# A two-layer hybrid trunk on one core: gate and GLU projections streamed 512 columns wide, first-layer tables built beside the transposes, output stages re-timed

## The chip, the cores and the metric

The kernel runs on one core of a Trainium2 chip. The metric is the device time of one execution in microseconds (us), lower is better. Four engines matter here: PE (TensorE, matrix products and 128x128 transposes), DVE (VectorE), ACT (ScalarE) and SP (SyncE, which issues the transfers). Every engine works through its own instructions strictly in the order in which the program lists them; an instruction that waits holds up all that stand behind it on its engine.

## What is computed

Two layers of the same form run on x, 256 positions by 2048 channels, in float32:

```python
for l in range(2):
    h = rmsnorm(x, pre_norm_g[l])
    proj = h @ w_in[l]                                  # 2048 x 6144
    q, k, v, z_att, u, z_ssm = split(proj)              # 1024 columns each
    o_att = rmsnorm(diff_attention(q, k, v)) * silu(z_att)
    y = s5_ssm(u, ...)                                  # a scan over the positions
    g_val, g_gate = split(gelu(y) @ w_glu[l])           # 1024 x 2048
    o_ssm = g_val * sigmoid(g_gate) * silu(z_ssm)
    x = x + rmsnorm(concat(o_att, o_ssm) @ w_out[l])    # 2048 x 2048
```

The state space branch takes four positions as one chunk. Tables made from its parameters lead from a chunk of u to the state (`wi`, the chunk-input table), through the state by 62 scan steps (`H`), and from the state to the outputs (`gc`, the output tables).

## The kernel before

All weights are streamed once. A layer's weights are cut into 144 **half chunks** of 128x1024 elements (`hs` in the code, `s` within a layer). Products are made at nearly float32 accuracy from two rounded parts: ACT copies a half chunk into `hi` (`emit_hi`), DVE subtracts that from the raw data into `lo` (`emit_lo`), and PE multiplies with three products (hi by hi, hi by lo, lo by hi) (`main`). The main loop, from line 1143, writes out for each half chunk s: the transfer of half chunk s+6, ACT's `hi` and DVE's `lo` of s+2, PE's products of s, and between them pieces of all other work. So `lo` of s+2 has to be finished by the time PE comes to s+2.

The segments of a layer, by half chunk: u 0 to 15, q 16 to 31, k 32 to 47, v and z_att 48 to 79, z_ssm (`zs`) 80 to 95, glu 96 to 111, out 112 to 143. There are two forms of product. In the segments u (mostly), q, k, zs and glu of the kernel before, a half chunk takes 24 products with 256 moving columns; the result has the channels on the partitions. In v, z_att and out, a half chunk takes 12 products with 512 moving columns, with the activations as the stationary side; the result has the positions on the partitions.

The other work is written as generators. Those in `gens` are advanced once per half chunk, either ahead of `lo` (`run_first`) or, where they yield a number, behind the products of the half chunk (`run_second`, with room 4). Operations on DVE that are long in sum stand in the queue `weave`, first in first out, and are let in between the two halves of `lo` by a budget in ns (`BUDS`, line 1111; `fill`, line 212): the parameters, `z_ops`, `g_ops` (12 operations that make the output tables) and `scan_ops` (62 steps of four operations).

The chain of the state space branch in layer 0: `prep_gen` (line 480) loads B and C, transposes C (`psc`), has `z_ops` made, transposes them to the chunk-input table (`psw`, one block of four transposes behind each of eight half chunks) and only then puts `g_ops` into the weave. `s_gen` waits for the table, makes the inputs of the scan (`pss`) and puts `scan_ops` into the weave behind `g_ops`. `y_gen` (line 742, four pieces j, started from half chunk `Y0` on) multiplies states by output tables (`psy`, `psz`), applies the GELU on ACT and DVE into a tile `y` of which there is one buffer, transposes it on PE (`psg`), and splits it to `ghi` and `glo`, the inputs of glu. `pv_gen` makes the attention output (`pwt`, `wt`, `po`). `evac` takes the finished sums of a segment out of PSUM; for zs and glu it does so once per 128 channels.

Of the kernel before, what the change touches and what calls it, by code (L numbers as in the profile page):

```python
# [27 lines left out]
Y0 = (78, 78)  # L28
# [30 lines left out]
def hybrid_trunk(ctx: ExitStack, tc, x, rel_bias, pre_norm_g, post_norm_g, w_in, lambda_q1, lambda_k1,  # L59
# [105 lines left out]
    for l in range(DEPTH):  # L165
# [13 lines left out]
    def emit_dma(hs):  # L179
# [300 lines left out]
    def prep_gen(l, slots, w_first):  # L480
# [13 lines left out]
        for _ in range(4):  # L494
            yield
# [26 lines left out]
        if not w_first:  # L522
            weave.append(g_ops(l, ccv, tcn, gslots))
# [17 lines left out]
        if not w_first:  # L541
            yield from until("g" + K)
        wi = []
        while l and not S["wfree"]:
            yield
        for b in range(8):
            if b % 4 == 0:
                wi.append(R(wslots[b // 4], "wi"))
            yield 1
            ps = side("psw")  # L550
            for pp in range(2):
                m = 4 * b + 2 * pp
                for a in range(2):
                    tpose(ps[:, 128 * (2 * pp + a):128 * (2 * pp + a) + 128],
                          zt[m // 16][:, 1024 * a + 64 * (m % 16):1024 * a + 64 * (m % 16) + 128], ident)
            yield
            psv = ps.rearrange("p (h a g q) -> p h a g q", h=2, a=2, g=2)
            wv = wi[b // 4].rearrange("p (b h r a q) -> p b h r a q", b=4, h=2, r=2, a=2)[:, b % 4]
            for r in range(2):
                for g in range(2):  # L560
                    act(wv[64 * g:64 * g + 64, :, r], psv[64 * r:64 * r + 64, :, :, g], AF.Copy)
            if l and b == WB - 1:
# [3 lines left out]
        if w_first:  # L566
            weave.append(g_ops(l, ccv, tcn, gslots))
# [174 lines left out]
    def y_gen(l, j):  # L742
        H, U = S["H"], S["U"]
        gc = S[f"gc{l}"][j // 2].rearrange("p (k q a c) -> p k q a c", k=4, q=4, a=2)[:, 2 * (j % 2):2 * (j % 2) + 2]
        yield from until(f"yt{l}{j - 1}" if j else f"h{l}")
        yield 2
# [30 lines left out]
        S[f"yt{l}{j}"] = True  # L777
        yield 1
# [112 lines left out]
    def evac(l, seg, b, ac):  # L891
# [13 lines left out]
        elif seg == "za":  # L905
# [5 lines left out]
            for t in range(2):  # L911
                c0 = 1024 * t + 512 * (b // 4)
                stt(S["za"][:, c0:c0 + 512], th[t], 1.0, ac[t], ALU.add, ALU.mult)
# [29 lines left out]
    def main(hs, only=None):  # L943
# [26 lines left out]
        elif seg in ("u", "q", "k", "zs"):  # L970
# [11 lines left out]
        elif seg == "glu":  # L982
            assert f"y{l}3" in S
            if h == 0:
                S["acc"] = [acc("acg")]
            o = S["acc"][0][:, 256 * h:256 * h + 256]
            hv = hi.rearrange("p (k c) -> p k c", k=8)
            lv = lo.rearrange("p (k c) -> p k c", k=8)
# [271 lines left out]
```

## Time and profile before

| | us |
|---|---|
| median of 3 runs | 942.68 (941.54 to 942.83) |
| profiled execution | 943.94 |
| its span in the trace | 942.2 |

The granted TensorE clock was 0.994 over the span. Busy shares by the page: PE 98%, weight loads 89%, DVE 74%, ACT 52%. The recorded length of a product is not what it costs in a stream: the next one starts before it ends, so costs on PE are read here from start to start.

### The profile page before, as it was taken

To read this page: it belongs to the slowest core of one execution; us is meant where nothing else is said; L and a number is where in the kernel's file an instruction comes from. 1 tells how busy PE (TensorE), PEld (TensorE's weight loads), DVE (VectorE), ACT (ScalarE), POOL (GpSimd) and SP (SyncE) were. 2 spreads that over 40 slices of the span, in tenths; PEclk is the share of its full clock that TensorE was granted. 3 is DMA by queue.
4 is the path that set the end of the run, shared out by engine and by line. 5 is a ranking of instruction groups with operands and counts; after the bars stand their busy time and mean duration, and the time that the engine had idled before them with its cause. 6 is when DMAs were issued, how large, how long until landed. Compare 5 with 4: busy or idle time off the path is not lost.

```text
span 942.2 us, 19053 instructions
## 1 busy us (share of the span) xinstructions
PE 921.2 (98%) x7458; PEld 841.5 (89%) x7458; DVE 694.0 (74%) x1653; ACT 489.4 (52%) x887; POOL 17.2 (2%) x26
## 2 busy tenths in 40 slices
PE   9999999999999999999999999999999999999995
PEld 8999999878789999888889999998888989998884
DVE  4898549899996756887877439999966566665564
ACT  6633375454356557444469343335565655744451
POOL 3000000000000000000000000000000000000001
PEclk9999999999999999999999999999999999999998
DMA  9988665545554498667646856665555446575862
GB/s 299 211 247 221 193 197 168 180 148 166 168 161 129 128 199 240 188 197 268 219 160 192 235 161 184 194 185 162 174 160 178 123 128 180 165 233 183 275 194 89
DMA packets 230458, 176.24 MB, mean 187 GB/s; under 512 B 36471, under 2 KB 190641, under 8 KB 229473
## 3 DMA queue, kind: packets, MB, share of 16 engines
q1 hardware_dynamic: 230016, 174.90, 63.0%
q8 instruction: 58, 0.95, 0.4%
q14 instruction: 32, 0.25, 0.1%
q0 software_dynamic: 352, 0.13, 0.1%
HBM read 167.39 MB, written 7.88 MB: 186 GB/s over the span
## 4 chain that ended last, share of the span: by engine, by line
PE 86%; DVE 7%; ACT 2%; SPq 1%; DMA 1%; issue 1%; DVEq 0%; ACTq 0%
PE ac L113 68%; PE acg L113 9%; DVE lo L116 3%; PE pss L113 2%; DVE sc L116 1%; PE acu L113 1%; PE lga L113 1%; PE po L113 1%; DMA raw<-in_w_in_dram 1%; SPq L489 1%; PE psy L113 1%; PE psw L97 1%; DMA cn<-in_ssm_c_re_dram 1%; ACT hi L134 0%; DVE y L123 0%
## 5 line engine op out<-in xcount | busy, mean ns | idle before, releaser
L134 ACT ACTIVATE hi<-raw 128x1024 fp32r<-128x1024 f32 (+1 forms) x282 | 297.3, 1057 | 366.9 <-PE ac L113 292.7
L116 DVE TENSOR_TENSOR lo<-raw,hi 128x512 fp32r<-128x512 f32 (+1 forms) x400 | 360.3, 904 | 112.4 <-ACT hi L134 111.3
L113 PE MATMUL ac<-hthi,hi 128*128 128x256 f32 x992 | 286.3, 289 | 0.0
L113 PE MATMUL ac<-htlo,hi 128*128 128x256 f32 x992 | 281.6, 284 | 0.2
L113 PE MATMUL ac<-hthi,lo 128*128 128x256 f32 x992 | 281.4, 284 | 0.0
L113 PEld LDWEIGHTS ac<-hthi,hi 128*128 128x128 f32 x992 | 191.1, 193 | 1.3 <-ACT hthi L134 0.3
L113 PEld LDWEIGHTS ac<-htlo,hi 128*128 128x128 f32 x992 | 191.2, 193 | 0.7 <-DVE htlo L123 0.7
L113 PEld LDWEIGHTS ac<-hthi,lo 128*128 128x128 f32 x992 | 190.9, 192 | 0.0
L113 PE MATMUL ac<-lo,hthi 128*128 128x512 f32 x256 | 100.6, 393 | 2.4 <-DVE lo L116 2.4
L113 PE MATMUL ac<-hi,hthi 128*128 128x512 f32 x256 | 102.4, 400 | 0.0
L113 PE MATMUL ac<-hi,htlo 128*128 128x512 f32 x256 | 100.0, 391 | 0.0
L113 PE MATMUL ac<-hi,mxhi 128*128 128x512 f32 x228 | 88.8, 390 | 0.0
L113 PE MATMUL ac<-lo,mxhi 128*128 128x512 f32 x228 | 88.7, 389 | 0.0
L113 PE MATMUL ac<-hi,mxlo 128*128 128x512 f32 x228 | 88.7, 389 | 0.0
L113 PE MATMUL acg<-ghi,hi 128*128 128x256 f32 x256 | 73.7, 288 | 0.0
L113 PE MATMUL acg<-ghi,lo 128*128 128x256 f32 x256 | 72.7, 284 | 0.6 <-DVE lo L116 0.4
L113 PE MATMUL acg<-glo,hi 128*128 128x256 f32 x256 | 72.4, 283 | 0.0
L113 PEld LDWEIGHTS ac<-lo,hthi 128*128 128x128 f32 x256 | 48.1, 188 | 14.9 <-DVE lo L116 5.8
L113 PEld LDWEIGHTS ac<-hi,hthi 128*128 128x128 f32 x256 | 48.1, 188 | 11.1
L113 PEld LDWEIGHTS ac<-hi,htlo 128*128 128x128 f32 x256 | 48.0, 188 | 10.2
L113 PEld LDWEIGHTS ac<-hi,mxlo 128*128 128x128 f32 x228 | 42.8, 188 | 8.9
L113 PEld LDWEIGHTS ac<-lo,mxhi 128*128 128x128 f32 x228 | 42.8, 188 | 8.8
(206 smaller groups left out, 1246.6 us busy)
## 6 DMA issues: line engine op xcount, KB each, us to landing
raw<-in_w_in_dram SPq DMA_DIRECT2D x191, 512.0 KB, 3.9
raw<-in_w_out_dram SPq DMA_DIRECT2D x64, 512.0 KB, 4.7
raw<-in_w_glu_dram SPq DMA_DIRECT2D x32, 512.0 KB, 4.6
xt<-in_x_dram SPq DMA_DIRECT2D x8, 256.0 KB, 7.3
uds<-u SPq DMA_DIRECT2D x4, 512.0 KB, 5.4
U<-uds SPq DMA_DIRECT2D x32, 64.0 KB, 2.4
pg<-in_post_norm_g_dram SPq DMA_DIRECT2D x2, 1024.0 KB, 6.1
xt<-in_x_dram SPq DMA_DIRECT2D x2, 1024.0 KB, 9.8
```

Source lines behind the costliest of these rows:

```text
L97: P.transpose(o, i, idn)
L113: P.matmul(o, lhsT=l, rhs=r, start=start, stop=stop, skip_group_check=True)
L116: V.tensor_tensor(o, a, b, op=op)
L134: A.activation(out=o, in_=i, func=f, **kw)
L489: SY.dma_start(out=bv[:, a], in_=src[l].rearrange("(m g) p c -> (g p) m c", g=2))
```

## The change

- zs and glu use the 512-column form. zs is taken out of PSUM like z_att, by two ACT and two DVE operations of 512 columns per 512 channels. glu takes the gate half first (two tanh of 512 columns), then the value half (two DVE operations); its result has the positions on the partitions and is therefore transposed by eight transposes (`psm`) per 512 channels, four times in the program, before it is split to `mxhi` and `mxlo`.
- glu's half chunks need only the piece of `ghi` and `glo` that belongs to their rows, no longer all four.
- In layer 0 the C transposes (`psc`) stand two half chunks later; `g_ops` are put into the weave before the chunk-input table's transposes, which come in four blocks of eight (two PSUM tiles at a time) instead of eight blocks of four.
- `y_gen` has one more step between the GELU and the transposes `psg`, and one more before its first piece; it starts at half chunk 80 in layer 0 (78 before) and 77 in layer 1 (78 before).
- The weave's budget in layer 0 is 2100 from half chunk 44 on instead of 2250.

```diff
-Y0 = (78, 78)
+Y0 = (80, 77)
...
-        if seg in ("u", "q", "k", "zs"):
+        if seg in ("u", "q", "k"):
...
-            c0 = 1024 * (1 - h) + 128 * b
-            src = w_glu_v[l][:, :, c0:c0 + 128]
+            k0, c0 = 4 * (b % 2) + 2 * h, 1024 * (1 - b // 2 % 2) + 512 * (b // 4)
+            src = w_glu_v[l][:, k0:k0 + 2, c0:c0 + 512]
...
-        for _ in range(4):
+        for _ in range(4 if l else 6):
             yield
...
-        if not w_first:
+        if l:
             yield from until("g" + K)
+        else:
+            weave.append(g_ops(l, ccv, tcn, gslots))
...
-        for b in range(8):
-            if b % 4 == 0:
-                wi.append(R(wslots[b // 4], "wi"))
-            yield 1
-            ps = side("psw")
+        nb = 1 if l else 2
+        for b0 in range(0, 8, nb):
+            if b0 % 4 == 0:
+                wi.append(R(wslots[b0 // 4], "wi"))
+            yield nb
+            pss = [side("psw") for _ in range(nb)]
...
         yield from until(f"yt{l}{j - 1}" if j else f"h{l}")
+        if not j:
+            yield
         yield 2
...
         S[f"yt{l}{j}"] = True
+        yield
         yield 1
         pg = side("psg")
...
-        elif seg == "za":
+        elif seg in ("za", "zs"):
...
-        elif seg == "zs":
-            z = tmp("z")
-            th = tmp("thz")
-            mul(z, ac[0][:, 0:256], rbc)
-            act(th, z, AF.Tanh, scale=0.5)
-            yield
-            stt(S["zs"][:, 256 * b:256 * b + 256], th, 1.0, z, ALU.add, ALU.mult)
+                stt(S[seg][:, c0:c0 + 512], th[t], 1.0, ac[t], ALU.add, ALU.mult)
...
-            th = tmp("thg")
-            act(th, ac[0][:, 0:256], AF.Tanh, scale=0.25)
-            yield
-            stt(th, th, 1.0, S["zs"][:, 256 * b:256 * b + 256], ALU.add, ALU.mult)
-            stt(th, ac[0][:, 256:512], 0.125, th, ALU.mult, ALU.mult)
-            act(S["mxhi"][:, 8 + b], th, AF.Copy)
-            yield
-            tt(S["mxlo"][:, 8 + b], th, S["mxhi"].bitcast(F32)[:, 8 + b], ALU.subtract)
+            n = b // 4
+            if b % 4 == 1:
+                S["th"] = [tmp5("thg") for _ in range(2)]
+                for t in range(2):
+                    act(S["th"][t], ac[t], AF.Tanh, scale=0.25)
+                yield
+                for t in range(2):
+                    c0 = 1024 * t + 512 * n
+                    stt(S["th"][t], S["th"][t], 1.0, S["zs"][:, c0:c0 + 512], ALU.add, ALU.mult)
+            else:
+                g = S["th"]
+                for t in range(2):
+                    stt(g[t], ac[t], rst[:, 1, t:t + 1], g[t], ALU.mult, ALU.mult)
+                yield
+                for p in range(2):
+                    yield 1
+                    ps = side("psm")
...
+                            tpose(ps[:, 256 * i + 128 * t:256 * i + 128 * t + 128], g[t][:, c:c + 128], ident)
...
+                    act(S["mxhi"][:, k:k + 2], psv, AF.Copy, scale=0.25)
+                    stt(S["mxlo"][:, k:k + 2], psv, 0.25, S["mxhi"].bitcast(F32)[:, k:k + 2], ALU.mult, ALU.subtract)
...
-            bal = min(bal, CAP) + BUDS[l] + pload[0] - load[0] - 1130
+            bal = min(bal, CAP) + (BUDL if not l and s >= 44 else BUDS[l]) + pload[0] - load[0] - 1130
```

Three places show how this stands on the engines. The first is PE in layer 0 behind half chunk 34, where `psw` are the transposes of the chunk-input table and `psu` those of another table; a piece of the difference between the two programs:

```order
 L113 MATMUL ac<-htlo,hi 128x256
 L113 MATMUL ac<-hthi,lo 128x256
-L97 MATMUL psw<-ident,zb 128x128 x4
+L97 MATMUL psw<-ident,zb 128x128 x8
 L97 MATMUL psu<-ident,t0t 128x128 x4
 L113 MATMUL ac<-hthi,hi 128x256
```

The blocks of eight stand behind half chunks 34 to 37, where blocks of four stood behind 34 to 41; the products `pss` that follow stand behind 38 to 41 instead of 42 to 45.

The second is DVE in layer 0 from the last operation on the table `t0t` on (about half chunk 35). Before:

```order
L116 TENSOR_TENSOR t0t<-t0t,ztmp 128x8x16
L116 TENSOR_TENSOR lo<-raw,hi 128x1024 x2
L123 SCALAR_TENSOR_TENSOR k<-ac,rbc 128x256
...
L116 TENSOR_TENSOR lo<-raw,hi 128x1024 x2
L123 SCALAR_TENSOR_TENSOR k<-ac,rbc 128x256
L116 TENSOR_TENSOR gc<-bt,apow 128x16x64
L116 TENSOR_TENSOR lo<-raw,hi 128x512
```

Of the change:

```order
L116 TENSOR_TENSOR t0t<-t0t,ztmp 128x8x16
L116 TENSOR_TENSOR gc<-bt,apow 128x16x64
L116 TENSOR_TENSOR lo<-raw,hi 128x512
L116 TENSOR_TENSOR ztmp<-bt,apow 128x1024
L116 TENSOR_TENSOR lo<-raw,hi 128x512
L116 TENSOR_TENSOR gc<-gc,ztmp 128x16x64
```

The output tables moved ahead by eight half chunks (the first from behind the `lo` of 43 to behind that of 35); the first scan operation stands behind the `lo` of 44 instead of 48, the last behind that of 84 instead of 81.

The third is ACT in layer 1 at half chunks 80 to 82, where attention output (`wt`, the two squares into `junk`) and the second piece of `y` meet. Before:

```order
L134 ACTIVATE wt<-pwt 128x384
L134 ACTIVATE hi<-raw 128x1024
L134 ACTIVATE ghi<-psg 128x4x128
L134 ACTIVATE junk,as<-po 128x128 x2
L134 ACTIVATE wt<-pwt 128x384
L134 ACTIVATE hi<-raw 128x1024
L134 ACTIVATE thz<-z 128x256
L134 ACTIVATE junk,as<-po 128x128 x2
L134 ACTIVATE wt<-pwt 128x384
L134 ACTIVATE y<-psy 128x16x16 x2
```

Of the change:

```order
L134 ACTIVATE junk,as<-po 128x128 x2
L134 ACTIVATE wt<-pwt 128x384
L134 ACTIVATE y<-psy 128x16x16 x2
L134 ACTIVATE y<-psz 128x16x16 x2
L134 ACTIVATE hi<-raw 128x1024
L134 ACTIVATE ghi<-psg 128x4x128
L134 ACTIVATE junk,as<-po 128x128 x2
L134 ACTIVATE y<-y 128x512
L134 ACTIVATE wt<-pwt 128x384
```

The second piece's copies into `y` stand one half chunk earlier, ahead of the split `ghi` of the first piece, and the third `wt` has the copies, `ghi` and the tanh `y<-y` in front of it.

## Rows read from the trace of the kernel before

**Rows 1.** The page, section 1: busy time, share, instructions.

```profile
PE 921.2 (98%) x7458; PEld 841.5 (89%) x7458; DVE 694.0 (74%) x1653; ACT 489.4 (52%) x887; POOL 17.2 (2%) x26
```

**Rows 2.** PE's waits: who waited for whom, total us, times, longest.

```profile
PE psg L97 <- DVE y L123: 2.9, 3, 1.8
PE ac L113 <- DVE lo L116: 2.4, 6, 0.7
...
PE psc L97 <- DMA cn<-in_ssm_c_re_dram: 1.1, 1, 1.1
PE po L113 <- ACT wt L134: 1.1, 1, 1.1
...
PE acg L113 <- DVE lo L116: 0.4, 1, 0.4
```

**Rows 3.** Timeline of PE, start, length, instruction: 256 columns, layer 0.

```profile
86.10 0.28 PE L113 MATMUL ac<-htlo,hi 128*128 128x256 f32 x1
...
90.06 0.28 PE L113 MATMUL ac<-htlo,hi 128*128 128x256 f32 x1
```

**Rows 4.** Timeline of PE: 512 columns, out segment of layer 1.

```profile
856.10 0.39 PE L113 MATMUL ac<-hi,mxhi 128*128 128x512 f32 x1
...
861.99 0.39 PE L113 MATMUL ac<-hi,mxlo 128*128 128x512 f32 x1
```

**Rows 5.** Timeline of PE around four transposes, layer 0.

```profile
126.82 0.60 PE L97 MATMUL psw<-ident,zb 128*128 128x128 f32 x4
...
127.38 0.28 PE L113 MATMUL ac<-htlo,hi 128*128 128x256 f32 x1
```

**Rows 6.** Busy time by stretch: us, then PE, PEld, DVE, ACT, POOL, clock, DMA.

```profile
109.00:153.90 44.90, 44.90 (x583) 44.27 (x581) 25.18 (x30) 28.76 (x51) 0.22 (x1) 1.00 0.67 195
153.90:207.70 53.80, 53.64 (x402) 44.93 (x401) 50.07 (x169) 25.45 (x52) 0.52 (x1) 1.00 0.51 157
207.70:273.30 65.60, 63.38 (x302) 50.17 (x300) 63.59 (x239) 31.16 (x63) 0.00 (x0) 1.00 0.55 167
362.00:375.20 13.20, 12.62 (x102) 12.01 (x101) 8.73 (x14) 9.82 (x22) 0.00 (x0) 1.00 0.73 230
```

**Rows 7.** Timeline of DVE: first and last of the 12 `g_ops`, layer 0.

```profile
143.93 1.22 DVE L116 TENSOR_TENSOR gc<-bt,apow 128x1024 f32<-128x1024 f32 x1
...
161.56 1.22 DVE L123 SCALAR_TENSOR_TENSOR gc<-gc,ztmp 128x1024 f32<-128x1024 f32 x1
```

**Rows 8.** Groups on DVE, 169.9 to 281 us: count, busy us, mean ns.

```profile
L116 DVE TENSOR_TENSOR sc<-H,apow 128x64 f32<-128x64 f32 x60 | 16.5, 275 | 1.2
```

**Rows 9.** Timeline of DVE and PE at half chunks 7 to 10, layer 0.

```profile
34.36 0.63 PE L97 MATMUL psc<-ident,cn 128*128 128x128 f32 x4 [1.08 <-DMA cn<-in_ssm_c_re_dram]
...
41.30 2.04 DVE L116 TENSOR_TENSOR u<-ac,rbc 128x256 f32<-128x256 f32 x4
```

**Rows 10.** Timeline of PE: waits in the y pieces of both layers.

```profile
286.56 0.94 PE L113 MATMUL po<-v,wt 128*128 128x128 f32 x6 [1.06 <-ACT wt L134]
...
315.87 0.66 PE L97 MATMUL psg<-ident,y 128*128 128x128 f32 x4 [0.73 <-DVE y L123]
...
768.85 0.66 PE L97 MATMUL psg<-ident,y 128*128 128x128 f32 x4 [1.78 <-DVE y L123]
```

**Rows 11.** Timeline of ACT, layer 1, y pieces and attention output.

```profile
735.03 0.66 ACT L134 ACTIVATE y<-psy 128x256 f32<-128x256 f32 x2 [0.79 <-PE psz L113]
...
740.15 0.63 ACT L134 ACTIVATE y<-y 128x512 f32<-128x512 f32 x1
740.67 0.49 ACT L134 ACTIVATE wt<-pwt 128x384 f32<-128x384 f32 x1
741.12 1.06 ACT L134 ACTIVATE hi<-raw 128x1024 fp32r<-128x1024 f32 x1
742.25 1.11 ACT L134 ACTIVATE ghi<-psg 128x512 fp32r<-128x512 f32 x1
...
743.70 0.49 ACT L134 ACTIVATE wt<-pwt 128x384 f32<-128x384 f32 x1
```

More of the change, by code (lines that the diff above doesn't have):

```diff
@@ L477, in params_ops, with prep_gen @@
         S["lam"] = True
-    def prep_gen(l, slots, w_first):
+    def prep_gen(l, slots):
         K = f"{l}"
@@ L540, in prep_gen @@
         S["cmfree" + K] = True
-        if not w_first:
+        if l:
             yield from until("g" + K)
+        else:
+            weave.append(g_ops(l, ccv, tcn, gslots))
         wi = []
@@ L545, in prep_gen @@
             yield
-        for b in range(8):
-            if b % 4 == 0:
-                wi.append(R(wslots[b // 4], "wi"))
-            yield 1
-            ps = side("psw")
[L551 to L555, printed above, removed]
-            yield
[L557 to L562, printed above, removed]
+        nb = 1 if l else 2
[4 more added lines that the diff above has]
+            pss = [side("psw") for _ in range(nb)]
+            for b, ps in zip(range(b0, b0 + nb), pss):
+                for pp in range(2):
+                    m = 4 * b + 2 * pp
+                    for a in range(2):
+                        tpose(ps[:, 128 * (2 * pp + a):128 * (2 * pp + a) + 128],
+                              zt[m // 16][:, 1024 * a + 64 * (m % 16):1024 * a + 64 * (m % 16) + 128], ident)
+            yield
+            for b, ps in zip(range(b0, b0 + nb), pss):
+                psv = ps.rearrange("p (h a g q) -> p h a g q", h=2, a=2, g=2)
+                wv = wi[b // 4].rearrange("p (b h r a q) -> p b h r a q", b=4, h=2, r=2, a=2)[:, b % 4]
+                for r in range(2):
+                    for g in range(2):
+                        act(wv[64 * g:64 * g + 64, :, r], psv[64 * r:64 * r + 64, :, :, g], AF.Copy)
+            if l and b0 == WB - 1:
                 for _ in range(WY):
@@ L969, in main @@
             done = b == 3 and h == 1
-        elif seg in ("u", "q", "k", "zs"):
+        elif seg in ("u", "q", "k"):
             if h == 0:
@@ L981, in main @@
             done = h == 1
[L982 to L988, printed above, removed]
-            gh = S["ghi"].rearrange("p (b c) -> p b c", b=8)
-            gl = S["glo"].rearrange("p (b c) -> p b c", b=8)
-            for k in range(8):
-                mm(o, hv[:, k], gh[:, k], k == 0, False)
-                mm(o, hv[:, k], gl[:, k], False, False)
-                mm(o, lv[:, k], gh[:, k], False, k == 7)
-            done = h == 1
-        else:
-            if b % 4 == 0 and h == 0:
+        else:
+            nb = 2 if seg == "glu" else 4
+            if b % nb == 0 and h == 0:
                 S["acc"] = [acc("ac0"), acc("ac1")]
@@ L1000, in main @@
             lv = lo.rearrange("p (k c) -> p k c", k=2)
-            ah, al = (S["mxhi"], S["mxlo"]) if seg == "out" else (S["hthi"], S["htlo"])
-            done = b % 4 == 3 and h == 1
+            if seg == "glu":
+                assert f"y{l}{(2 * b + h) % 4}" in S
+                ah, al = (S[n].rearrange("p (k c) -> p k c", k=8) for n in ("ghi", "glo"))
+            else:
+                ah, al = (S["mxhi"], S["mxlo"]) if seg == "out" else (S["hthi"], S["htlo"])
+            done = b % nb == nb - 1 and h == 1
+            kl = 4 * nb - 1
             if only is not None:
@@ L1008, in main @@
             for kk, t in order:
-                k = 4 * (b % 4) + 2 * h + kk
+                k = 4 * (b % nb) + 2 * h + kk
                 o = S["acc"][t]
@@ L1111, in hybrid_trunk @@
     BUDS = (2250.0, 2200.0)
+    BUDL = 2100.0
     with tc.manual_schedule():
@@ L1139, in hybrid_trunk @@
         at(PG, params_gen())
[L1140 removed]
+        at(2, prep_gen(0, (3, (1, 7), (4, 8))))
         S["done"] = None
```

13 lines of the change are left out of this document (7 added, 6 removed).

## The prediction

> **What bounds the kernel now.** I read the page's busy times first [rows 1]: PE is busy 98% of the span, DVE 74%, ACT 52%. A busy PE alone does not say that PE is the limit, so I read its waits next [rows 2]. They are few: PE stood for the y pieces three times (2.9 us), for `lo` six times (2.4), for a transfer of C once (1.1), for attention weights `wt` once (1.1), and once at glu (0.4). The rest of the listed rows are start-up and the layer boundary, which the change leaves alone. So the time is PE's stream of products, end to end, plus some 8 us of waits at known places. A change pays if it shortens that stream or takes out one of these waits, and costs if PE comes to wait somewhere else.
>
> What a product costs is the distance from start to start. With 256 columns 33 products lie between the two rows: 3.96 us, 0.120 each [rows 3]. With 512 columns 26 lie between: 5.89 us, 0.2265 each [rows 4]. A wait costs PE a little more than its idle time: the product before it is recorded 0.39 long but would have been followed after 0.23, so 0.16 is added to each. The stretches show where DVE is short [rows 6]: in layer 0 it is busy 25.2 of 44.9 us in half chunks 32 to 43, then 50.1 of 53.8 and 63.6 of 65.6 in half chunks 44 to 79. There the six waits for `lo` lie.
>
> **The change part by part.** I sum against the profiled execution (943.94, span 942.2); the median of the runs is 1.26 lower, and I take the differences off the median.
>
> *The 512 form.* zs and glu have 16 half chunks each in each layer, 64 in all; 24 products of 0.120 (2.88 us) become 12 of 0.2265 (2.72 us). Over 64 half chunks, 1536 products for 184.3 us become 768 for 174.0: **-10.3 us**, all on PE and so all on the path, as long as `hi` and `lo` keep up with 2.72 us. In the out segment they do; in glu the other work is denser (below).
>
> The Trainium skill, page "TensorE: Matmul & The Clock Gate", section "Back-to-back issue gap", gives the isolated distance as N/2.4 + 2.5 ns, that is 109.2 ns for 256 columns and 215.8 for 512. By it two narrow products cost only 2.6 ns more than a wide one, and the form would save an estimated 2.0 us instead of 10.3. The trace has 120.0 and 226.5, 13.5 ns more per extra product, and I take the trace.
>
> *The transposes of glu.* Eight per 512 channels, four times, 32 in all. Four transposes in the stream took 0.44 us (from 126.82 to 127.38, less one product of 0.120) [rows 5], so 0.11 each: **+3.5 us**. The longest four are recorded as 0.66 [rows 10], which gives 5.3 as the upper end. I take 3.5, since the row in the stream is the same block between the same kind of products. Their inputs come from DVE one half chunk earlier, at a place where DVE has slack.
>
> *Evacuation of zs and glu.* Fewer, wider operations on ACT and DVE over the same elements or less; neither is on the path in these segments except as in the next point. The multiplication on DVE ahead of zs's tanh goes. Cost nothing; if the cover were gone, one 512-column operation would be late by its length, 0.6 to 0.7.
>
> *Glu of layer 0.* PE was idle 0.6 of 13.2 us in 362 to 375 [rows 6], waiting for `lo`, which waited for `hi`, because ACT also makes layer 1's tables there. The tanh and the copies for glu are gathered into two half chunks of four; ACT has less to do in the others. I take **-0.8** of the 0.6 plus the tails of the waits; bounds 0 and -1.1.
>
> *Output tables ahead, scan sooner, smaller budget (layer 0).* Twelve operations of about 1.14 us (1.22 long) stood from 143.93 to 161.56 [rows 7]; about half of them, 6.8 us, leave the stretch in which DVE is full and go to the one where it was idle for 19.7 us. The scan's 248 operations, at most 0.275 each [rows 8], spread over 40 half chunks instead of 33: at most 2.1 us of a half chunk become 1.7, and some 6.8 us fall behind half chunk 79. DVE's 113.7 of 119.4 us there become about 100. So the six waits for `lo` go: 2.4 + 6 x 0.16 = **-3.4**. Bounds 0 and -4. What is queued behind: the first y piece needs the end of the scan. It now stands behind half chunk 84, and the last scan operation comes right after the `lo` of 84, that is before PE begins 84; PE has a whole half chunk in hand.
>
> The chunk-input table's transposes are only regrouped: eight times four become four times eight. On ACT the copies of two PSUM tiles fall on each of four half chunks; ACT had 28.8 of 44.9 us to do there. I cost it at nothing; if ACT fell behind, PE would wait about 1 us for a PSUM tile.
>
> *`psc` two half chunks later.* The wait for C was 1.08 + 0.16 [rows 9]. When it goes, the next late thing is the `lo` of half chunk 10: DVE has the four operations on u ahead of it (41.30 + 2.04, less 0.1 to 0.2 of overlap) and then about 1.1 for `lo` (1024 elements, as in rows 7), ready at about 44.3. PE came to it at about 45.2: 34.36, four blocks of transposes, three half chunks of 2.88 and one product of the norm, about 0.5. Without the wait and with two of the blocks still to come, it would be there at 43.1 and stand for its third product until 44.3. So of 1.2 us about 0.8 is given back: **-0.4**; bounds 0 and -1.2. Nothing moves on SP's queue; the transfers of C are issued where they were.
>
> *y pieces.* PE's three waits at `psg` were for the GELU's last operation on DVE [rows 10]: 2.9 + 0.5 = **-3.4** when one more half chunk lies between. The wait of `po` (1.06 + 0.16, for `wt`, which stood on ACT behind zs's tanh and y's copies) goes as well, since the attention of layer 0 is now past that place before the first y piece: **-1.2**.
>
> *A new wait.* There is one buffer of `y`. With the later transposes, the next piece's copies into it now stand on ACT ahead of them in time and wait for them; behind the copies stand `hi`, `ghi`, two squares, the tanh and `wt`. In layer 1 `wt` is needed soon. From the end of the products of half chunk 81: ACT waits 0.44, then copies 1.1 (2 x 0.55), `hi` 1.1, `ghi` and squares 1.45, tanh 0.52, `wt` 0.45 [rows 11], 5.1 in all. PE takes 0.44 + 0.94 (`po`, as in rows 10) + 0.33 (`pwt`, three transposes) + 2.72 until it wants `wt`: 4.4. So PE stands about 0.6 + 0.16 = **+0.8**; bounds 0 and +2.
>
> The sum: -10.3 + 3.5 - 0.8 - 3.4 - 0.4 - 3.4 - 1.2 + 0.8 = -15.2. 942.68 - 15.2 = **927.5 us** (928.7 for a profiled execution, a span of about 927).
>
> **The rivals.** *The waits move and do not go* (the re-timing does not do what it says): DVE's work and ACT's stay the same in sum, so the waits for `lo`, for y and at glu could come up a few half chunks on. Against it speaks the idle DVE in rows 6. 3.4 + 3.4 + 0.8 us back: 935.1. *The wide form saves nothing*: with glu's and zs's operands the distance grows to two narrow ones, 0.240, and the 10.3 us are not there: 937.8. Rows 3 and 4 speak against it, from the same kernel with operands of the same kind. (The page's formula comes near this case; by it an estimated 2.0 us would stay and the time would be 935.8.) *ACT behind `psg`* (slower): in each layer three pieces of y make ACT wait for transposes that stand behind a half chunk of products. If ACT's work between two such waits is longer than PE's, `hi` comes late and PE stands for a half chunk and the transposes, 2.72 + 0.44 = 3.2, at six places: +19, 946.5. It decides where ACT's work (two `hi` 2.1, copies 1.1, tanh 0.5, `ghi` 0.9, and 1.2 for zs, 5.8) exceeds PE's two half chunks, transposes and the `psy` products (over 5.9). It is close to that only where zs is taken out. *Everything clears*: no new wait, the whole wait for C, and the small gaps between products that a full DVE makes, some 2 us: 924.
>
> **How the numbers follow.** Forecast as summed 0.70; waits move 0.12; wide form saves nothing 0.04; ACT behind `psg` 0.05; everything clears 0.09. The unknown costs (transposes +1.8, new wait -0.8 to +1.2, C -0.8 to +0.4, table copies +1, glu -0.3 to +0.8) make the forecast's own range about 924.5 to 931. The range reaches to the clear case and most of the way to the moved waits: 923.0 to 934.5. A measurement of this kernel can tell 0.2%, 1.9 us, from no change. Faster by more: all cases but the ACT rival and a little of the rest, 0.94; within 0.2%: 0.02; slower: 0.04.
>
> **What would show it.** Right: products 0.2265 apart in zs and glu of the profile after; `psm` blocks of eight about 0.9 long; no wait of PE for `lo` in layer 0 between half chunks 48 and 79; no wait at `psg`; a wait for `wt` of about a microsecond at half chunk 82 of layer 1; DVE near 85% in half chunks 44 to 79. Wrong: products further apart in zs or glu; waits for `hi` or `lo` in the y stretch (the ACT rival); PE standing at the first `psy` for the scan; or a wait for PSUM at the blocks of eight.

## The result: 930.05 us, and the profile after

| | before | changed |
|---|---|---|
| median | 942.75 (941.54 to 943.09, 4 runs) | 930.05 (929.27 to 930.50, 4 runs) |
| profiled execution, its span | 943.94, 942.2 | 930.50, 928.7 |

The ratio of the runs is 0.9876 with a 95% interval of 0.9865 to 0.9888, so the change saves 1.1 to 1.4%. The medians are 12.7 us apart where 15.2 were forecast.

The page's busy times and PE's waits (us in total, times, longest) answer to [rows 1, 2]:

```profile
PE 914.6 (98%) x6722; PEld 803.8 (87%) x6722; DVE 685.6 (74%) x1607; ACT 485.9 (52%) x863; POOL 17.2 (2%) x26
```
```profile
PE ac L113 <- DVE lo L116: 0.8, 2, 0.6
PE po L113 <- ACT wt L134: 0.5, 1, 0.5
```

The other rows of the list belong to the start and the layer boundary. The waits at `psg`, at `psc` and at glu are gone, the six for `lo` in half chunks 48 to 79 too. Two others stand in their place, both waits of more than 0.5 us (the list's second wait for `lo`, 0.17 us, lies at 317.8 us, in zs of layer 0). One was forecast: `po` waits for `wt` in layer 1. The timelines of ACT and PE there (start, length, instruction, idle time before it and what ended it) show the copies of the second y piece waiting for the first piece's transposes, and PE's wait behind them:

```profile
737.58 0.66 ACT L134 ACTIVATE y<-psy 128x256 f32<-128x256 f32 x2 [4.31 <-PE psg L97]
...
741.54 0.52 ACT L134 ACTIVATE wt<-pwt 128x384 f32<-128x384 f32 x1
```
```profile
742.12 0.49 PE L113 MATMUL po<-v,wt 128*128 128x128 f32 x2 [0.52 <-ACT wt L134]
```

The other was not forecast. It is a wait for `lo` in the out segment of layer 0 (1.2 us with its tail and a shorter stop ahead of it). DVE's timeline there, and PE's product that waits:

```profile
423.06 1.29 DVE L123 SCALAR_TENSOR_TENSOR mg<-ac,pg 128x512 f32<-128x512 f32 x2 [4.20 <-ACT junk L134]
...
424.79 1.22 DVE L116 TENSOR_TENSOR gc<-bt,apow 128x1024 f32<-128x1024 f32 x1
425.92 0.69 DVE L116 TENSOR_TENSOR lo<-raw,hi 128x512 fp32r<-128x512 f32 x1
...
428.26 1.22 DVE L116 TENSOR_TENSOR gc<-gc,ztmp 128x1024 f32<-128x1024 f32 x1
429.40 2.36 DVE L116 TENSOR_TENSOR lo<-raw,hi 128x1024 fp32r<-128x1024 f32 x2
```
```profile
430.68 0.50 PE L113 MATMUL ac<-lo,mxhi 128*128 128x512 f32 x1 [0.61 <-DVE lo L116]
```

DVE idles 4.2 us, and then the evacuation `mg` and layer 1's tables (`t0t`, left out here, and `gc`) come at once, ahead of and between the halves of `lo`. The next `lo` begins only at 429.40, and what DVE idled before does not help.

The forms on PE are as forecast. Products with 512 columns, and a block of eight transposes `psm`, in PE's timeline of glu:

```profile
356.87 0.39 PE L113 MATMUL ac<-lo,ghi 128*128 128x512 f32 x1
357.10 0.40 PE L113 MATMUL ac<-hi,glo 128*128 128x512 f32 x1
357.33 1.04 PE L97 MATMUL psm<-ident,thg 128*128 128x128 f32 x8
358.12 0.48 PE L113 MATMUL ac<-hi,ghi 128*128 128x512 f32 x1
358.44 0.39 PE L113 MATMUL ac<-lo,ghi 128*128 128x512 f32 x1
```

From 357.10 to 358.12 less one product are 0.79 us before the first product, and that one is followed after 0.32 instead of 0.23: 0.88 in all.

DVE in half chunks 44 to 79 of layer 0 (columns as in [rows 6]) is not what was forecast:

```profile
157.30:217.00 59.70, 59.70 (x324) 50.19 (x323) 58.32 (x213) 29.63 (x54) 0.52 (x1) 1.00 0.62 189
217.00:267.70 50.70, 50.70 (x253) 41.57 (x251) 48.55 (x181) 27.30 (x57) 0.00 (x0) 1.00 0.57 173
```

It is busy 106.9 of 110.4 us, 97%, fuller than before (113.7 of 119.4), and yet PE does not wait. The stretch is 9 us shorter: 4.6 of that are PE's waits and delays, and 4.5 are the products `pss`, which now stand ahead of half chunk 44.

### The profile page after: what moved, and what is told of

The parts are those of the page before. It is cut to its first block, busy times and chain, and to the rows that moved or that the text cites. A ratio compares the mean times of both kernels' runs of the same rounds, so it can differ in the third digit from the quotient of the medians.

```text
span 928.7 us, 17559 instructions
## 1 busy us (share of the span) xinstructions
PE 914.6 (98%) x6722; PEld 803.8 (87%) x6722; DVE 685.6 (74%) x1607; ACT 485.9 (52%) x863; POOL 17.2 (2%) x26
## 4 chain that ended last, share of the span: by engine, by line
PE 92%; DVE 3%; ACT 3%; DMA 2%; issue 1%; SPq 0%; DVEq 0%; ACTq 0%
PE ac L113 82%; PE pss L113 2%; DMA xt<-in_x_dram 1%; PE lga L113 1%; PE po L113 1%; PE psy L113 1%; PE psw L97 1%; ACT hi L134 1%; DVE lo L116 1%; ACT junk L134 1%; PE acu L113 1%; PE pwt L97 0%; DMA raw<-in_w_in_dram 0%; PE pst L113 0%; ACT hthi L134 0%
## 5 line engine op out<-in xcount | busy, mean ns | idle before, releaser
L113 PE MATMUL ac<-hthi,hi 128*128 128x256 f32 x736 | 212.2, 288 | 0.0
L113 PE MATMUL ac<-htlo,hi 128*128 128x256 f32 x736 | 209.5, 285 | 0.2
L113 PE MATMUL ac<-hthi,lo 128*128 128x256 f32 x736 | 209.2, 284 | 0.1
L113 PE MATMUL ac<-hi,hthi 128*128 128x512 f32 x384 | 154.3, 402 | 0.0
L113 PE MATMUL ac<-hi,htlo 128*128 128x512 f32 x384 | 150.0, 391 | 0.0
L113 PE MATMUL ac<-lo,hthi 128*128 128x512 f32 x384 | 149.8, 390 | 0.2 <-DVE lo L116 0.2
L113 PEld LDWEIGHTS ac<-hthi,hi 128*128 128x128 f32 x736 | 142.2, 193 | 0.9 <-ACT hthi L134 0.3
L113 PEld LDWEIGHTS ac<-htlo,hi 128*128 128x128 f32 x736 | 142.3, 193 | 0.7 <-DVE htlo L123 0.7
L113 PEld LDWEIGHTS ac<-lo,mxhi 128*128 128x128 f32 x228 | 42.8, 188 | 10.3 <-DVE lo L116 1.5
L113 PE MATMUL ac<-hi,ghi 128*128 128x512 f32 x128 | 51.5, 403 | 0.0
L113 PE MATMUL ac<-hi,glo 128*128 128x512 f32 x128 | 50.1, 392 | 0.0
```

Of the source, the lines that this page charges most:

```text
L113: P.matmul(o, lhsT=l, rhs=r, start=start, stop=stop, skip_group_check=True)
```

## The experiments

Every variant was run beside the kernel before on the same chip. The three parts of the change are called the form (zs and glu 512 wide), the tables (output tables ahead, scan sooner, `psc` later, budget) and the y steps. The table gives the ratio to before with its 95% interval:

| variant | median, us | ratio |
|---|---|---|
| changed kernel, again | 930.57 | 0.9882 [0.9864, 0.9899] |
| form alone | 933.95 | 0.9915 [0.9901, 0.9929] |
| tables alone | 939.17 | 0.9971 [0.9961, 0.9981] |
| y steps alone | 945.41 | 1.0041 [1.0027, 1.0054] |
| form and tables | 929.79 | 0.9877 [0.9859, 0.9895] |
| form and y steps | 934.39 | 0.9926 [0.9914, 0.9939] |
| before without `z` | 939.38 | 0.9970 [0.9958, 0.9983] |
| changed, budget to half chunk 111 | 928.32 | 0.9857 [0.9844, 0.9871] |
| changed, two buffers of `y` | 928.08 | 0.9854 [0.9838, 0.9869] |
| changed, `psc` early | 929.49 | 0.9871 [0.9850, 0.9891] |
| changed, `psm` twice | 932.43 | 0.9901 [0.9888, 0.9915] |
| changed, with the edits on budget, `y` and `psc` | 925.51 | 0.9829 [0.9816, 0.9843] |

And this one says where the time went: the time between PE's first products of the half chunks named, less the same of before, in the profiled executions (us):

| half chunks | changed | form | tables | y steps | form, tables | form, y steps | changed, with the three edits |
|---|---|---|---|---|---|---|---|
| start and 0 to 15, layer 0 | -1.1 | -1.3 | -0.4 | -1.0 | -0.8 | -1.8 | -1.9 |
| 16 to 47 | 0 | 0 | 0 | 0 | 0 | 0 | 0 |
| 48 to 79 | -4.6 | -0.1 | -4.6 | -0.1 | -4.6 | -0.1 | -4.6 |
| 80 to 95 | -3.9 | -3.1 | -1.7 | +1.9 | -3.6 | -1.5 | -4.3 |
| 96 to 115 | -1.7 | -1.8 | 0.1 | +1.6 | -1.8 | -1.8 | -1.7 |
| 116 to 143 | +1.3 | 0 | +1.8 | 0 | +1.3 | 0 | 0 |
| 0 to 3, layer 1 | 0 | -1.5 | -1.2 | -1.5 | -1.5 | -1.5 | -1.5 |
| 80 to 95 | -3.3 | -3.1 | 0 | +0.5 | -3.1 | -3.3 | -4.3 |
| 96 to 115 | -0.3 | -0.3 | 0 | 0 | -0.3 | -0.3 | -0.3 |

The stretches left out are within 0.2, but for one of +0.9 in half chunks 4 to 79 of layer 1 with the tables alone; there transposes of layer 1's own table (`psw`) have moved out of half chunks 0 to 3, whose -1.2 in that column belongs to it. Each column is one profile against one profile. A second profile of the changed kernel agrees with the first within 0.04 in every row but two: the first row (-0.7 instead of -1.1) and half chunks 0 to 3 of layer 1 (-1.5 instead of 0). That second row is not work of the change (last section), and the profile of before is an unlucky one in both: it has the late C in the first and the lower clock in the other.

### The form alone

```diff
-        if seg in ("u", "q", "k", "zs"):
+        if seg in ("u", "q", "k"):
...
-            c0 = 1024 * (1 - h) + 128 * b
-            src = w_glu_v[l][:, :, c0:c0 + 128]
+            k0, c0 = 4 * (b % 2) + 2 * h, 1024 * (1 - b // 2 % 2) + 512 * (b // 4)
+            src = w_glu_v[l][:, k0:k0 + 2, c0:c0 + 512]
...
-        elif seg == "za":
+        elif seg in ("za", "zs"):
```

> The kernel before with the 512-column form of zs and glu (and the transposes of glu) alone. Theory (products 0.2265 instead of 2 x 0.120 apart, -10.3; 32 transposes, +3.5; some +0.06 more for each side block in a 512-column stream, about +0.7; the wait at glu of layer 0 gone, -0.4 to -0.8): about 936, that is -6.5 to -7.5. Rival A, the form saves nothing and the whole gain of the change comes from the tables and the re-timing: 945 to 946 (the transposes alone remain). Rival B, the form saves but its wide evacuations hold up `lo` where the y pieces stand at their old places: 938 to 941, with new waits of PE for `hi` or `lo` in half chunks 80 to 111. The waits for `lo` in half chunks 48 to 79 (2.4) and at `psg` (2.9) must stay in this kernel.

Measured: 933.95, so 8.0 us of the gain, and no rival; but it is 2 us below the theory, and the theory's last sentence failed. PE's waits in this kernel:

```profile
PE ac L113 <- DVE lo L116: 2.2, 5, 0.7
...
PE psg L97 <- DVE y L123: 1.4, 3, 0.6
...
PE po L113 <- ACT wt L134: 0.5, 1, 0.5
```

The waits for `lo` are those of before [rows 2], as expected, but those at `psg` and `po` fell by more than half, and the one at glu went, with nothing re-timed. Counted from start to start these waits are 5.6 us in the zs and glu segments of before and 2.5 here. So 3.1 of the 8 us are waits, and the form itself is worth about 5.

### The tables alone

```diff
-        for _ in range(4):
+        for _ in range(4 if l else 6):
...
-        if not w_first:
+        if l:
             yield from until("g" + K)
+        else:
+            weave.append(g_ops(l, ccv, tcn, gslots))
...
-            bal = min(bal, CAP) + BUDS[l] + pload[0] - load[0] - 1130
+            bal = min(bal, CAP) + (BUDL if not l and s >= 44 else BUDS[l]) + pload[0] - load[0] - 1130
```

> The kernel before with the first layer's part alone: output tables made ahead of the chunk-input table's transposes, blocks of eight, scan begun sooner, `psc` two half chunks later, weave budget 2100 from half chunk 44 of layer 0 on. Theory: the six waits for `lo` go (-3.4 to -4.5), `psc` gives -0.4 to -1.0, and the out segment of layer 0 pays +1.3 for tables that now stand right beside the evacuation `mg`; sum 938.5 to 940. Rival A, the waits move on and do not go: 942 to 943. Rival B, the wait at `po` goes too because the later scan's end puts the first y piece behind the attention of layer 0: 937 to 938.

Measured: 939.17, within the theory by the median, but not by its terms. Half chunks 48 to 79 give the whole 4.6, and half chunks 80 to 95 another 1.7, since the wait at `po` went too (rival B's mechanism): it is not in this kernel's list of waits.

```profile
PE psx L97 <- issue: 1.9, 1, 1.9
...
PE ac L113 <- DVE lo L116: 1.2, 2, 1.0
```

The 1.8 us in half chunks 116 to 143 were not the expected wait for `lo` beside `mg`. PE stood 1.9 us at the layer boundary. The list names no releaser ("issue"), but DVE's timeline there shows one:

```profile
468.54 1.22 DVE L123 SCALAR_TENSOR_TENSOR gc<-gc,ztmp 128x1024 f32<-128x1024 f32 x1
469.67 0.15 DVE L1023 TENSOR_REDUCE nv<-sso 128x1 f32<-128x5 f32 x1
```
The last operation on layer 1's tables stands right ahead of the norm's first operation `nv`, whose row of small operations ends in `xt` (at 471.40, 0.75 long), which `psx` transposes (at 472.26). In before the tables end in half chunk 139, four half chunks ahead of the boundary, and DVE idles 1.1 us before `nv`; here they stand in 132 to 143. So with narrow forms the late tables cost their time at the boundary. That the smaller budget, which stays in force there, is what makes them late was not run with narrow forms.

The two waits for `lo` lie in the first half chunks (at 8.6 and 44.0 us); the second, 1.0 us, is the price of the later `psc`.

### The y steps alone

```diff
-Y0 = (78, 78)
+Y0 = (80, 77)
...
+        if not j:
+            yield
         yield 2
...
         S[f"yt{l}{j}"] = True
+        yield
         yield 1
         pg = side("psg")
```

> The kernel before with the y pieces re-timed alone (one step more ahead of `psg`, one more ahead of the first piece, starts at half chunks 80 and 77). Theory: the three waits at `psg` (2.9 and 0.5 of tails) and the wait at `po` (1.2) go, a wait for `wt` of 0.8 to 1.5 comes in layer 1: 939 to 940. Rival, ACT behind `psg`: with zs still in 256 columns ACT has its old work and waits at each piece's copies for the transposes of the piece before, so that `hi` comes late: 941 to 944, with waits of PE for `hi`.

Measured: slower, 945.41. The theory fell. The rival named the place, ACT's copies, but not the size (941 to 944) nor what came late: it was `wt` and some `lo`, not `hi`. PE's waits, and ACT's and PE's timelines in layer 1:

```profile
PE po L113 <- ACT wt L134: 3.8, 2, 2.3
...
PE psg L97 <- DVE y L123: 0.7, 1, 0.7
```
```profile
748.47 0.66 ACT L134 ACTIVATE y<-psy 128x256 f32<-128x256 f32 x2 [4.38 <-PE psg L97]
...
751.97 0.42 ACT L134 ACTIVATE thz<-z 128x256 f32<-128x256 f32 x1 [1.35 <-DVE z L116]
...
754.35 0.48 ACT L134 ACTIVATE wt<-pwt 128x384 f32<-128x384 f32 x1
```
```profile
754.88 0.82 PE L113 MATMUL po<-v,wt 128*128 128x128 f32 x5 [2.29 <-ACT wt L134]
```

The waits at `psg` do shrink, from 2.9 to 0.7. But the copies of the next piece wait 4.4 us for the transposes, and behind them on ACT stands zs's tanh `thz`, which waits once more, for `z` on DVE. `wt` is then 2.3 us late, where the changed kernel has 0.5. The other wait for `wt`, 1.5 us at 280.0 in layer 0, comes before any copy into `y`; it is the one that the form with the y steps shows again (below).

### Budget only up to half chunk 111

```diff
-            bal = min(bal, CAP) + (BUDL if not l and s >= 44 else BUDS[l]) + pload[0] - load[0] - 1130
+            bal = min(bal, CAP) + (BUDL if not l and 44 <= s < 112 else BUDS[l]) + pload[0] - load[0] - 1130
```

> The changed kernel with the weave's budget of 2100 only up to half chunk 111 of layer 0 (2250 behind it, as before). In the changed kernel PE waited for `lo` twice (1.0 us, with tails 1.3) at 428 to 431 us in layer 0, where layer 1's tables `t0t` and `gc` stand on DVE in the same half chunk as the two evacuations `mg`. Theory, the smaller budget pushed the tables two half chunks back onto `mg`: with it lifted the two waits go, 928.7 to 929.2 (-0.9 to -1.3 against the changed kernel). Rival, DVE is full there anyway (the wide glu has put its own work there): the waits turn up a few half chunks on, 930.

Measured: 928.32. The interval overlaps that of the changed kernel, but the trace is plain: half chunks 116 to 143 cost 0.0 more than before instead of 1.3, and PE has no wait there. (In glu of layer 0 0.5 of it comes back as a wait for `lo`.) DVE's timeline at the same place:

```profile
423.60 1.29 DVE L123 SCALAR_TENSOR_TENSOR mg<-ac,pg 128x512 f32<-128x512 f32 x2 [1.31 <-ACT junk L134]
424.81 1.22 DVE L116 TENSOR_TENSOR lo<-raw,hi 128x1024 fp32r<-128x1024 f32 x1
425.94 1.22 DVE L116 TENSOR_TENSOR gc<-bt,apow 128x1024 f32<-128x1024 f32 x1
```

A whole `lo` stands between `mg` and the next table operation again, and the idle time ahead of `mg` is 1.3 instead of 4.2. The tables begin in half chunk 125 here and in 129 in the changed kernel. So the smaller budget beyond half chunk 111 caused the new wait, together with the place where the tables then meet `mg`: the tables alone have that budget and no such wait.

### The changed kernel again

> The changed kernel unaltered, beside its three variants of this group so that small differences are read on one chip: 930 again (ratio 0.987 to 0.988).

Measured: 930.57. It is the anchor for the next three.

### Two buffers of `y`

```diff
-    ty = ctx.enter_context(tc.tile_pool(name="ty", bufs=1))
+    ty = ctx.enter_context(tc.tile_pool(name="ty", bufs=2))
...
-        yt = ty.tile([128, 1024], F32, tag="y", name="y")
-        y, sq = yt[:, 0:512], yt[:, 512:1024]
+        y = ty.tile([128, 512], F32, tag="y", name="y")
+        sq = scp.tile([128, 512], F32, tag="ysq", name="ysq")
```

> The changed kernel with two buffers of `y` (its second half, the squares, in a buffer of its own, since that fits). In the changed kernel PE waited for `wt` at three places of layer 1 (0.28, 0.24 and 0.68 with tails, 1.2 in all), and ACT stood for 4.3 us before the second piece's copies into `y`, until PE had done the transposes `psg` of the first. Theory of the prediction, the one buffer makes the wait: the copies no longer wait, the three waits of PE go, -1.0 to -1.2 against the changed kernel, 928.8 to 929.1. Rival, `wt` is late because ACT has too much ahead of it there anyway: ACT's idle time moves elsewhere, PE's waits for `wt` stay at 0.8 or more, 929.8 to 930.2.

Measured: 928.08, -2.5 against the changed kernel of the same group by the medians (the two intervals just overlap). ACT's copies of the second piece now wait only for their own products:

```profile
733.45 0.39 ACT L134 ACTIVATE y<-psy 128x256 f32<-128x256 f32 x1 [0.89 <-PE psz L113]
```

Of PE's three stops for `wt` in layer 1 one of 0.28 (with its tail) is left. Half chunks 80 to 95 gain 0.5 more in layer 0 and 1.1 more in layer 1. So the one buffer made the wait, in both layers, and it is worth the 1.6 us of these stretches; the rest of the 2.5 is not in them.

### `psc` at its old place

```diff
-        for _ in range(4 if l else 6):
+        for _ in range(4):
```

> The changed kernel with `psc` where it stood before (behind half chunk 6 on instead of two later). The prediction priced the move at -0.4, so undoing it should cost +0.4: 930.4. The first group of runs speaks against that: with the old place, two kernels showed no wait for C at all, and PE took 26.2 us from half chunk 4 to half chunk 12 in both; with the new place it took 26.9 to 27.3 in three, since the `lo` of half chunk 10 then waits for the four operations on u. By that (theory now) undoing the move gains 0.7 to 1.0 where C is in time and nothing where it is late as in the profile of before: 929.1 to 930.

Measured: 929.49, too close to the changed kernel for its time to decide. The traces do better. With the early place, PE waited for C in one profile of seven, that of before [rows 9]. With the late place, all seven profiles are longer from half chunk 4 to 15, by 0.2 to 1.2 us, than the six early ones in which C was in time. PE stood for the `lo` of half chunk 10 in six of the seven, for up to 1.00 us (the tables alone). The next, in the changed kernel run again, on DVE and PE:

```profile
40.60 2.03 DVE L116 TENSOR_TENSOR u<-ac,rbc 128x256 f32<-128x256 f32 x4
42.47 1.21 DVE L116 TENSOR_TENSOR lo<-raw,hi 128x1024 fp32r<-128x1024 f32 x1
```
```profile
43.74 0.38 PE L113 MATMUL ac<-hthi,lo 128*128 128x256 f32 x1 [0.85 <-DVE lo L116]
```

### The form and the tables, without the y steps

```diff
-Y0 = (80, 77)
+Y0 = (78, 78)
...
-        if not j:
-            yield
         yield 2
...
         S[f"yt{l}{j}"] = True
-        yield
         yield 1
```

> The changed kernel without the re-timing of the y pieces (no further steps in them, starts at 78 in both layers): the wide form and the first layer's part alone. By the prediction's terms the re-timing is worth 3.4 + 1.2 - 0.8 = 3.8 us: 933.9, with waits of 2.5 to 3 us at `psg`. Rival, formed from the first group of runs: the wide form alone already halves the waits at `psg` (2.9 to 1.4) and at `po` (1.1 to 0.5), because ACT and DVE have less to do for zs there; then the re-timing adds only 0.5 to 1.5: 930.5 to 931.5, with 0.8 to 1.5 us at `psg`.

Measured: 929.79 beside 930.57 of the changed kernel, below both; the rival is the nearer, and the y steps are worth nothing that the times show. In the traces they give 0.3 and 0.1 in half chunks 80 to 95 of the two layers. PE waits 1.7 us at `psg` here and not at all for `wt`; with the y steps it is the other way round.

```profile
PE psg L97 <- DVE y L123: 1.7, 3, 0.6
```

### `psm` twice

```diff
-                    for i in range(2):
+                    for i in (0, 0, 1, 1):
                         for t in range(2):
```

> The changed kernel with each of glu's 32 transposes `psm` made twice, the second on top of the first. The block of eight took 0.89 us from start to start in the profile, 0.11 a transpose, though each is recorded as 0.27 and more. Theory, a transpose in the stream costs its distance: +3.5 us, 933.8 (ratio 0.991). Rival, it costs its recorded length: +8.7, 939. Rival, part of it lies beside other work: under +2.

Measured: 932.43, about +2: by the time the last rival, but the stages show the theory. In layer 1, where nothing else moved, half chunks 96 to 115 take 1.74 us more for 16 transposes: 0.109 each. In layer 0 they take 2.5 more, some of it a new wait for `lo`, and the out segment takes 1.3 less: layer 1's tables begin in half chunk 126 instead of 129, and the wait beside `mg` went. So the price per transpose is the distance, as taken, and the recorded length (0.27) is not.

### The form and the y steps, without the tables

```diff
-        for _ in range(4 if l else 6):
+        for _ in range(4):
...
-        if l:
+        if not w_first:
             yield from until("g" + K)
-        else:
-            weave.append(g_ops(l, ccv, tcn, gslots))
...
-            bal = min(bal, CAP) + (BUDL if not l and s >= 44 else BUDS[l]) + pload[0] - load[0] - 1130
+            bal = min(bal, CAP) + BUDS[l] + pload[0] - load[0] - 1130
```

> The changed kernel without the first layer's part (output tables, scan, budget, `psc` as before): the wide form and the re-timed y pieces. By the stages of the other traces: half chunks 48 to 79 of layer 0 lose their gain (+4.6), the out segment of layer 0 its new waits (-1.3), the old place of `psc` gives -0.3 to -1.0, half chunks 80 to 95 of layer 0 between 0 and +2 (the scan ends sooner, and y meets the attention): 932.3 to 936, likeliest 934. Rival, y re-timed without the later scan brings the waits of that kernel that had the re-timing alone (+2 to +5 in half chunks 80 to 95 of layer 0): 936 to 940.

Measured: 934.39, the likeliest value. PE's waits:

```profile
PE ac L113 <- DVE lo L116: 2.7, 8, 0.7
PE po L113 <- ACT wt L134: 2.1, 2, 1.6
```

In half chunks 80 to 95 of layer 0 the y steps cost 1.6 against the form alone: `po` stands 1.6 for `wt`. It is not the wait that y's copies made in before. On ACT and PE:

```profile
276.06 0.40 ACT L134 ACTIVATE att<-att,mx 128x128 f32<-128x128 f32 x1 [1.95 <-DVE mx L816]
```
```profile
279.30 0.38 PE L113 MATMUL po<-v,wt 128*128 128x128 f32 x1 [1.59 <-ACT wt L134]
```

ACT stood 1.95 us for the maximum `mx` of the attention, which DVE made behind `lo` and scan steps, and `wt` stands behind that, at 278.78. With the form alone ACT has the same wait, but PE has the first y piece's products there (from 278.16 on), so that it does not come to `po` too early; the y steps take this cover away. With the tables DVE has `mx` done in time at that place (ACT does not wait for it), and PE does not wait either.

### Before, without `z`

```diff
-            z = tmp("z")
+            z = ac[0][:, 0:256]
             th = tmp("thz")
-            mul(z, ac[0][:, 0:256], rbc)
```

> The kernel before, narrow forms and old places throughout, with one operation left out: DVE's multiplication `z` ahead of zs's tanh (so z_ssm lacks the norm's factor, and the output is not the reference's). In the trace of before the tanh of the y piece stood on ACT behind `thz`, which waited 1.96 us for `z` on DVE (at 767.1 us), and PE's longest wait at `psg` (1.78) followed. Theory: that multiplication, not the place of the transposes, made the waits at `psg`: they fall from 2.9 to 1.4 or less, as in the kernel with the wide form alone, the time by 1.5 to 2.5: 939.5 to 940.5. Rival, the waits fall in the wide form because ACT has fewer operations: no change here, 2.9 at `psg`, 941.5 to 942.3.

Measured: 939.38, and the waits:

```profile
PE psg L97 <- DVE y L123: 0.7, 2, 0.4
...
PE po L113 <- ACT wt L134: 0.2, 1, 0.2
```

The waits at `psg` fall from 2.9 to 0.7 and that at `po` from 1.1 to 0.2, with all forms and places of before. DVE's `z` and ACT's timeline in before, ahead of the longest wait at `psg` (768.85 in [rows 10]), and ACT at the same place without `z`:

```profile
766.68 0.42 DVE L116 TENSOR_TENSOR z<-ac,rbc 128x256 f32<-128x256 f32 x1
767.13 0.42 ACT L134 ACTIVATE thz<-z 128x256 f32<-128x256 f32 x1 [1.96 <-DVE z L116]
767.45 0.61 ACT L134 ACTIVATE y<-y 128x512 f32<-128x512 f32 x1
```
```profile
761.94 0.37 ACT L134 ACTIVATE thz<-ac 128x256 f32<-128x256 f32 x1
762.20 0.62 ACT L134 ACTIVATE y<-y 128x512 f32<-128x512 f32 x1
```

The multiplication of 0.42 us stood on DVE behind two halves of `lo` and a row of small operations, zs's tanh waited for it, and the y piece's tanh stood behind that on ACT. Two more waits of before follow such a stop of ACT: it stood 1.90 us for `z` at 283.96, ahead of the wait at `po` at 286.56, and 2.39 at 310.56, ahead of the wait at `psg` at 315.87 [rows 10] (there a `lo` also stands ahead of the GELU's last operation on DVE). The third wait at `psg` (0.36, at 741.56) is there without `z` too. Leaving `z` out also takes its 0.42 us, sixteen times, off DVE; how much of the 2.2 us by the medians is due to that alone was not separated.

### The three edits together

The changed kernel with the edits of the experiments on the budget, on `y` and on `psc`.

> The changed kernel with two buffers of `y`, the smaller budget only up to half chunk 111 of layer 0, and `psc` at its old place. If the three gains add: -1.7 to -2.5 for y, -1.3 to -1.7 for the budget, -0.3 to -1.1 for `psc`: 925.5 to 926.8, with no wait of PE for `lo` in layer 0 between half chunks 48 and 143 and one short wait for `wt`. Rival, the waits move to one another's places: 927.5 to 928.5.

Measured: 925.51, ratio 0.9829 [0.9816, 0.9843], the fastest of all; it beats both kernels (its interval lies below that of the changed kernel, 0.9864 to 0.9899). The gains add: half chunks 80 to 95 are within 0.1 of what they are with two buffers, 116 to 143 as with the shorter budget, 4 to 15 as with the early `psc`; the 0.5 that the shorter budget alone lost in glu is not lost here. Of its waits those of the layer boundary (the first row) and the start (the other, a short one for `lo`, lies at 8.2 us) are left, and one of 0.28 with its tail for `wt`:

```profile
PE psx L97 <- DVE xt L123: 1.5, 1, 1.5
...
PE ac L113 <- DVE lo L116: 0.2, 1, 0.2
```

## Why the prediction was right, and where it was wrong

The time fell in the range, 2.5 us above the forecast, but not all of it for the reasons given. That it came so near is in part luck: the form brought 1.6 us less than summed and the budget cost 1.3 that the sum did not have, while the tables brought 1.2 more.

*The 512 form* was the main thing, as forecast. The nominal part is right: 768 products 0.2265 apart. The form alone is worth about 5.2 us net in the trace (8.36 in zs and glu, less 3.13 of waits) instead of 6.8, so the term was mis-sized by about 1.6. The small delays between products (each under 0.15) sum to 1.8 us in the 512 form of zs and glu where the 256 form had 0.4, and the product behind a `psm` block is followed after 0.32 (0.4 for the four blocks). I took the distance from the out segment, where the stream is quieter. In layer 1 the wide glu brings only 0.3 us: of the 2.6 that its products save, the sixteen transposes take back 1.7, and the small delays and the products behind the blocks most of the rest. The Trainium skill's isolated formula (page "TensorE: Matmul & The Clock Gate", section "Back-to-back issue gap") would have left an estimated 2.0 us of the 10.3, less than the 3.5 of the transposes; the form with its transposes saved 5.2, so the measurement decides against it here.

*Glu of layer 0* came out: the waits there, 1.05 us with their tails, are gone with the form (0.8 forecast).

*Output tables, scan, budget*: the six waits went, 4.6 us instead of 3.4, because small delays went with them. But the reason was half wrong. I had DVE fall to about 100 us of work there, 85%, and it has 106.9 of 110.4. The 6.8 us of tables left, as said. Of the scan 17 operations left (241 before, 224 after; 4.7 us instead of 6.8), since what ended later also began sooner, and 3.5 us of `lo` and attention came in their place. The stretch itself is 9 us shorter. So DVE is as full as before and no longer late. Whether the tables' going or the smaller budget did that was not separated.

*The budget's other end* was overlooked. The line says `s >= 44` with no upper end, so it also holds in the out segment, where layer 1's tables are woven. The prediction costed it only up to half chunk 79. It took 1.3 us there, and the experiment with an end at 111 gives them back (0.5 of it is lost again in glu). With the tables alone, layer 1's tables were pushed to the layer boundary and cost 1.8.

*`psc`*: wrong in sign for the usual execution. The wait for C of 1.08 [rows 9] came from one profile and was not in six others with the same place. The second half of the step, that `lo` of half chunk 10 becomes late, came true (up to 1.00), and without a gain on the other side it is a loss. The sum was too kind by its own figures as well: from 43.1 to 44.3, less the two products that stand ahead of the third, PE waits 1.0 and not 0.8. That the two profiles compared here gain 1.0 in half chunks 4 to 15 is luck: a late C in the one, a nearly punctual `lo` in the other.

*y pieces*: the step that failed. Their terms came out (the waits at `psg` and that at `po` in layer 0 are gone), but the cause was taken wrongly. I blamed the place of the transposes, and in the part on evacuation I costed the loss of zs's multiplication "at nothing". In fact that multiplication was the head of the chain: without it, in the old order, the waits at `psg` are 0.7. The wide form, which drops it too, has 1.4 to 1.7 there at the old places, so the place has a share. And `po` in layer 0 went with the tables, as the prediction also said, not by the y steps: with the tables and old places it is gone, with the y steps but without the tables it is 1.6. What the y steps themselves do is exchange 1.7 us at `psg` for the three stops for `wt`.

*The new wait* was foreseen in the right place with the right cause, 1.2 instead of 0.8 in layer 1. Its share in layer 0, where a second buffer gives 0.5 more, was missed.

*ACT behind `psg`*, the slower rival, is real where zs is still narrow: with the y steps alone ACT waits over 4 us at the copies in both layers, and zs's tanh waits behind them. It is a part of the 3.5 us by which that kernel is slower; 1.5 us of them are the wait for `wt` that has another cause. The prediction named the right condition ("only where zs is taken out"). The changed kernel has the waits of ACT too (4.3 us), but no `hi` comes late by them: what is left is the new wait above.

## What to carry to other kernels

A wait is caused by the head of the chain that ends in it, not by the last instruction named: follow what the engine before it stood for, and price the removal of a small operation that others wait behind. A re-timing that gives one engine a half chunk more needs a buffer for what now lives longer; with one buffer it only moved the wait here. A budget that is lowered for one stage should end with that stage, and a wait for a transfer seen in one profile should be looked for in a second before it is priced.

## What the runs showed of the hardware

Behind the layer boundary the granted clock fell in some executions and not in others. The same two stretches of before and then of the form alone (columns as in [rows 6]):

```profile
476.00:479.90 3.90, 2.41 (x21) 2.01 (x19) 2.93 (x13) 1.61 (x5) 0.00 (x0) 1.00 0.18 67
479.90:483.00 3.10, 2.95 (x13) 2.67 (x13) 2.80 (x7) 3.08 (x8) 0.00 (x0) 0.59 0.26 93
```
```profile
469.60:473.60 4.00, 2.51 (x21) 2.11 (x19) 3.04 (x13) 1.60 (x5) 0.00 (x0) 1.00 0.20 69
473.60:476.70 3.10, 2.95 (x22) 2.67 (x22) 2.80 (x7) 3.08 (x8) 0.00 (x0) 1.00 0.22 85
```

PE is busy 2.4 to 2.5 us of the 4 ahead in both, with the same wait of 1.5 for `xt`. Then the clock is at the lower level of 1.2 GHz for most of 3 us in the one and stays at 2.4 in the other; 256-column products lie 0.21 apart instead of 0.12. It costs 1.5 us. Five of the fourteen profiles have it (before, changed, the tables alone, two buffers of `y`, before without `z`), and it is not a matter of the program: the second profile of the changed kernel does not. The half chunks 0 to 3 of layer 1 in the table are this; the sum of the prediction is not touched, since the profiles of both kernels have it.
